# Sums of weights and low parts of activations made by accumulating DMAs, in a transformer block that multiplies in three passes

## The chip, the cores and the metric

The kernel runs on one core of one Trainium2 chip. The metric is the device time of one execution in microseconds; the time before is the median of three runs. The core has TensorE (PE, with its weight loads PEld), VectorE (DVE), ScalarE (ACT), GpSimd (POOL) and SyncE (SP), and 16 DMA engines that carry out the transfers which SP, ACT and POOL issue.

## What is computed

One encoder block on 256 tokens of width 2048, all in float32 (cut to what matters here):

```python
proj = x @ w_in                       # retention q, k, v, gate; latent q, kv, rope key
mix  = concat(retention(proj), latent_attention(proj)) @ w_out
x1   = layer_norm(ALPHA * x + mix, ln1_g, ln1_b)
h    = square(relu(x1 @ w_up)) @ w_down        # w_up 2048 x 8192, w_down 8192 x 2048
out  = layer_norm(ALPHA * x1 + h, ln2_g, ln2_b)
```

The up product (`w_up`) and the down product (`w_down`) are where the change works. The third place with seven-product pairs, the retention projection, keeps its own way of building sums, apart from one sign.

## The kernel before

**Three products for one.** TensorE multiplies in a reduced-precision float32 format, `F32R`. Each operand is split into a high part (rounded to that format by ScalarE, line 389) and a low part, the rest (a subtraction on VectorE, line 390). A product is then high x high + high x low + low x high: three matmuls of 128 x 512, one after the other into the same accumulator. Weights arrive from DRAM 1 MB at a time in one of three `raw` buffers (loads issued by SP), and their high and low parts stand in five slots of 128 x 1024 (`hi`, `lo`). A raw buffer is loaded again when the weights three jobs back have been read; a slot is filled again when TensorE is done with it.

**Pairs.** A job is two 128-deep slices of a weight matrix, 1024 columns wide, against 256 tokens: a 2 x 2 block product (two slices, two halves of 512 columns, two halves of 128 tokens). Done plainly (`pair_products`, line 353) it takes eight products, 24 matmuls. Some jobs use Winograd's form of Strassen's scheme (`seven_products`, line 441): seven products, 21 matmuls, bought with sums of weights (`first`, `second`, `third` in `weights_pair`, lines 398, 404, 408, all VectorE) and sums of tokens (`token_sums`, lines 364 to 369). `SEVEN` lists which jobs of the two down passes are sevens, `UP_SEVEN` those of the up blocks: 2 in block 1 and 4 in each of blocks 2 to 7. Products that several outputs share gather in four more accumulators (`mb`), which `up_gather` and `add_sums` combine afterwards.

**Down passes.** The down product runs twice over all 32 pairs, once for each half of the output columns: pass 0, then pass 1 in another order of blocks. Two pairs use one block of 512 activations. `r_split` makes a block's high part `rhl[:, 0]` on ScalarE (line 1233) and its low part `rhl[:, 1]` on VectorE (line 1237); two such tiles take turns. Pass 0 writes the low part of blocks 0 to 13 to DRAM (`r_keep`, line 1243, a DMA on GpSimd's queue), and pass 1 reads it back (line 1235). Token sums of six pairs (`STORED`) made in pass 0 are kept for pass 1.

**Order.** The program is scheduled by hand: each engine executes in the order in which the code issues. While TensorE's work for a job is being written, `unit()` issues the next pieces of jobs to come (`next_piece`), as far as slots allow, in the order of `SEVEN_PARTS`: s0 token sums, s1 to s3 weight sums, w0 to w3 the splits. `load_ahead` issues the raw loads. So an instruction that waits on VectorE holds all later pieces on VectorE.

Of the kernel before, what the change touches and what calls it, by code (L numbers as in the profile page):

```python
# [14 lines left out]
P = 128  # L15
# [27 lines left out]

SEVEN_PARTS = ('s0', 's1', 'w0', 's2', 'w2', 's3', 'w1', 'w3')
X1_AT = ((1, 2), 1)
UP_STEP = 1
# [18 lines left out]
NSLOT = 5  # L65
LO_KEPT = range(14)
X_AFTER = {0: (1, 1), 1: (2, 2), 3: (4, 4), 6: (8, 4), 10: (12, 4)}

# [24 lines left out]
class Job:  # L93


    def __init__(self, load, pieces, slotted):
        self.load = load
        self.pieces = pieces
        self.slotted = slotted
        self.slots = None  # L100
        self.left = None
        self.seven = False
        self.held = False
# [8 lines left out]
def kernel(  # L112
# [44 lines left out]
    holders = []  # L157
    state = {"dma": 0, "job": 0, "unit": 0, "pause": 0, "heads": 0}
# [18 lines left out]
    def next_piece(force):  # L177
        while state["job"] < len(jobs) and not left(jobs[state["job"]]):
            state["job"] += 1
        if state["job"] == len(jobs):  # L180
            return False
        job = jobs[state["job"]]
        if job.held:
            return False
        load_ahead(state["job"])
        i = job.left[0]
# [174 lines left out]
    def token_sums(r0, r1, st, v):  # L361


        nc.vector.tensor_add(st[:, 0], r0[:, P:], r1[:, P:])
        nc.vector.tensor_sub(st[:, 1], st[:, 0], r0[:, 0:P])
        nc.vector.tensor_sub(st[:, 2], r0[:, 0:P], r0[:, P:])
        nc.vector.tensor_sub(st[:, 3], r1[:, 0:P], st[:, 1])
        nc.scalar.copy(v[:, :, 0], st)
        return lambda: nc.vector.tensor_sub(v[:, :, 1], st, v[:, :, 0].bitcast(F32))

    def weights_pair(name, load, half, columns, sums=None, seven=False, into=None):

# [23 lines left out]
        def first():  # L396
            a, b, t13 = columns(job, extra["t13"])
            nc.vector.tensor_sub(t13, a, b)
            if sums:
                job.rest()  # L400

# [4 lines left out]
        def third():  # L406
            b21 = half(job, 1, 0, 4)
            nc.vector.tensor_sub(shaped(extra["t4"], b21), b21, half(job, 0, 4, 8))

        job.load = lambda: load(job)  # L410
        job.seven = seven
        if not seven:
            job.pieces = [lambda e=e: split(e, half(job, e, 0, 8)) for e in range(2)]
            job.slots = [e if into is None or into[e] is None else None for e in range(2)]
        else:
            parts = {"s0": token_part, "s1": first, "s2": second, "s3": third,
                     "w0": lambda: split(0, half(job, 1, 0, 8)), "w1": lambda: split(1, half(job, 0, 0, 8)),
                     "w2": lambda: split(2, extra["t13"]), "w3": lambda: split(3, extra["t4"], 512)}
            job.pieces = [parts[p] for p in SEVEN_PARTS]
            job.slots = [int(p[1]) if p[0] == "w" else None for p in SEVEN_PARTS]  # L420
        job.hi, job.lo = [None] * 4, [None] * 4
# [7 lines left out]
    def seven_products(job, x, k, sums, cb, mb, first, last, done=None):  # L429
        for a, w, o, pb, alone in ((("x", 1, 0), 0, 0, cb[0][0], False), (("s", 3), 0, 512, cb[0][1], False),  # L430
                                   (("s", 0), 2, 0, mb[2], True), (("s", 2), 2, 512, mb[3], True),
                                   (("x", 0, 0), 1, 0, mb[0], True), (("s", 1), 1, 512, mb[1], True),
                                   (("x", 1, 1), 3, 0, cb[1][0], False)):
            use_slot(job, w)
# [7 lines left out]
            if o or w == 3:  # L442
                free(job, (w,))
                if done and w == 1:
                    side.append(done)
# [98 lines left out]
    def up_pair(b, kp):  # L544
        def load(job):
            raw = raw_tile(job, f"raw_wu{b}_{kp}")
            nc.sync.dma_start(raw.rearrange("p (f c) -> p f c", f=8),
                              w_up[8 * b:8 * b + 8, :, kp * 256:(kp + 1) * 256].rearrange("f p c -> p f c"))
# [4 lines left out]
        def columns(job, t):  # L553
            v = job.raw.rearrange("p (f e c) -> p f e c", f=8, e=2)
            return (v[:, 4:8].rearrange("p f e c -> p e f c"), v[:, :, 0].rearrange("p (j f) c -> p j f c", j=2),
                    t.rearrange("p (j f c) -> p j f c", j=2, c=P))

        return weights_pair(f"wu{b}_{kp}", load, half, columns, None, kp in UP_SEVEN[b])

    def down_pair(p, pair, into=None, seven=None):  # L560
        def load(job):
            raw = raw_tile(job, f"raw_wd{p}_{pair}")
            nc.sync.dma_start(raw.rearrange("p (e c) -> p e c", e=2),
                              w_down[2 * pair:2 * pair + 2, :, p * 1024:(p + 1) * 1024].rearrange("e p c -> p e c"))

        def half(job, e, i, j):
# [7 lines left out]

        def columns(job, t):
            return (job.raw.rearrange("p (e j c) -> p e j c", e=2, j=2)[:, :, 1],
                    job.raw[:, 0:1024].rearrange("p (j c) -> p j c", j=2), t.rearrange("p (j c) -> p j c", j=2))

        return weights_pair(f"wd{p}_{pair}", load, half, columns, None if seven is None or p == 1 and pair in STORED else sums, seven is not None, into)

# [645 lines left out]
    def r_split(b, keep=None):  # L1226
# [7 lines left out]
        if b in lo_kept:  # L1234
            nc.gpsimd.dma_start(t[:, 1].rearrange("p k t -> p (k t)"), lo_kept[b])
        else:
            nc.vector.tensor_sub(t[:, 1], r, t[:, 0].bitcast(F32))
# [71 lines left out]
    def up_gather(mb):  # L1309
# [9 lines left out]
        nc.vector.tensor_add(g[2], g[2], g[1])  # L1319
        nc.vector.tensor_add(g[1], g[1], g[3])  # L1320
        yield
        nc.vector.tensor_add(g[3], g[3], g[2])

# [72 lines left out]
    def add_sums(p, mb):  # L1396
# [13 lines left out]
        plus(0, 1, v)  # L1410
        nc.vector.tensor_add(v, v, p5)
        yield
        plus(1, 1, v)
        nc.vector.tensor_add(u, u, p5)
        yield
# [194 lines left out]
```

## Time and profile before

| what | value |
|---|---|
| median of 3 runs | 1100.75 us (1100.7 to 1100.85) |
| the profiled execution's own time | 1100.88 us |
| its span in the trace | 1099.1 us |
| granted TensorE clock | 0.999 |
| busy: PE, PEld | 1091.1 us (99%), 912.1 us (83%) |
| busy: DVE, ACT, POOL | 955.4 us (87%), 656.7 us (60%), 24.7 us (2%) |
| DMA moved | 231.78 MB, mean 211 GB/s |

The span is the time from the first to the last instruction of the program in the trace. In a timeline row the first number is the start in us from the span's beginning, the second how long the instruction (or the merged row) took; matmuls overlap in the pipeline, so what one costs is the distance from start to start. `u`, `v` and `d`, `s` are accumulators of up and down products, plain and shared; `t` and `ut` hold weight sums, `sx` token sums, `xm` the sums ahead of their split, `rr` the activations.

### The profile page before, as it was taken

The numbers are of one execution on the slowest core, as the hardware profiler recorded it, in microseconds if no ns is written. First come the engines' busy times: TensorE is split into PE (matmuls) and PEld (weight loads), VectorE is DVE, ScalarE is ACT, GpSimd is POOL, SyncE is SP. The second block draws the span as 40 slices with busy tenths as digits, with TensorE's granted clock in tenths as the row PEclk, the third lists the DMA queues.
The fourth block names the chain that finished last, engine by engine and source line by source line (L and its number), as shares of the span: only waits on it lengthen the run. The fifth ranks groups of instructions, "written<-read, shape, count | busy, mean of one in ns | idle before, by whom it ended". The sixth has DMA issues, their size and how long they took to land.

```text
span 1099.1 us, 13768 instructions
## 1 busy us (share of the span) xinstructions
PE 1091.1 (99%) x5145; PEld 912.1 (83%) x5145; DVE 955.4 (87%) x1304; ACT 656.7 (60%) x847; POOL 24.7 (2%) x46
## 2 busy tenths in 40 slices
PE   9999999999999999999999999999999999999997
PEld 8888888888888889888888888888888888888885
DVE  7878779889785777889999999999899999999985
ACT  4545556546463455467777677776666663666660
POOL 0000000000000000000000000000000000000000
PEclk9999999999999999999999999999999999999999
DMA  8655364535266544666656756757677876777792
GB/s 286 243 201 188 138 225 171 222 115 208 109 230 230 216 176 154 194 200 197 213 171 196 234 165 192 230 181 271 205 249 253 260 239 220 264 238 263 255 336 97
DMA packets 97026, 231.78 MB, mean 211 GB/s; under 512 B 4672, under 2 KB 63040, under 8 KB 89152
## 3 DMA queue, kind: packets, MB, share of 16 engines
q1 hardware_dynamic: 92496, 215.64, 57.6%
q0 software_dynamic: 4032, 14.68, 3.9%
q8 instruction: 40, 0.66, 0.2%
q10 hardware_dynamic: 432, 0.59, 0.2%
q14 instruction: 26, 0.21, 0.1%
HBM read 221.46 MB, written 9.44 MB: 210 GB/s over the span
## 4 chain that ended last, share of the span: by engine, by line
PE 97%; DVE 1%; DMA 1%; issue 0%; ACT 0%; POOL 0%; SPq 0%; DVEq 0%
PE d L353 21%; PE u L353 15%; PE r L353 12%; PE o L353 8%; PE v L441 6%; PE s L441 5%; PE u L441 5%; PE m L353 5%; PE d L441 4%; PE rs L441 2%; PE up L924 2%; PE pu L924 2%; PE r L441 1%; PE ut L1353 1%; PE pv L353 1%; PE up L930 1%
## 5 line engine op out<-in xcount | busy, mean ns | idle before, releaser
L353 PE MATMUL d<-hi_wd,rhl 128*128 128x512 f32 x632 | 174.7, 390 | 0.0
L390 DVE TENSOR_TENSOR lo_wd<-raw_wd,hi_wd 128x1024 fp32r<-128x1024 f32 x125 | 150.4, 1220 | 19.9 <-ACT hi_wd L389 19.5
L389 ACT CAST hi_wd<-raw_wd 128x1024 fp32r<-128x1024 f32 x125 | 129.3, 1051 | 56.1 <-DVE raw_wd L404 17.8
L390 DVE TENSOR_TENSOR lo_wu<-raw_wu,hi_wu 128x1024 fp32r<-128x1024 f32 x112 | 135.5, 1220 | 12.0 <-ACT hi_wu L389 10.9
L353 PEld LDWEIGHTS d<-hi_wd,rhl 128*128 128x128 f32 x632 | 118.4, 188 | 24.3
L389 ACT CAST hi_wu<-raw_wu 128x1024 fp32r<-128x1024 f32 x112 | 117.7, 1055 | 34.5 <-PE u L353 10.6
L353 PE MATMUL u<-hi_wu,x1hl 128*128 128x512 f32 x480 | 137.0, 394 | 0.0
L353 PE MATMUL r<-hi_ret,xhl 128*128 128x512 f32 x384 | 110.2, 397 | 0.0
L353 PEld LDWEIGHTS u<-hi_wu,x1hl 128*128 128x128 f32 x480 | 88.3, 188 | 17.2
L353 PE MATMUL d<-lo_wd,rhl 128*128 128x512 f32 x316 | 97.7, 389 | 0.0
L353 PEld LDWEIGHTS r<-hi_ret,xhl 128*128 128x128 f32 x384 | 71.0, 188 | 14.1
L390 DVE TENSOR_TENSOR lo_ret<-raw_ret,hi_ret 128x1024 fp32r<-128x1024 f32 x64 | 76.1, 1218 | 6.9 <-ACT hi_ret L389 6.7
L389 ACT CAST hi_ret<-raw_ret 128x1024 fp32r<-128x1024 f32 x64 | 65.9, 1052 | 25.6 <-PE r L353 14.7
L353 PE MATMUL u<-lo_wu,x1hl 128*128 128x512 f32 x240 | 74.2, 390 | 0.0
L353 PEld LDWEIGHTS d<-lo_wd,rhl 128*128 128x128 f32 x316 | 59.3, 188 | 12.4
L353 PE MATMUL r<-lo_ret,xhl 128*128 128x512 f32 x192 | 59.5, 391 | 0.0
L353 PE MATMUL o<-hi_wo,mix 128*128 128x512 f32 x208 | 57.5, 393 | 0.0
L441 PE MATMUL v<-hi_wu,us 128*128 128x512 f32 x156 | 56.5, 389 | 0.0
L353 PEld LDWEIGHTS u<-lo_wu,x1hl 128*128 128x128 f32 x240 | 45.0, 188 | 9.6
L441 PE MATMUL s<-hi_wd,sx 128*128 128x512 f32 x126 | 45.6, 389 | 0.0
L353 PEld LDWEIGHTS o<-hi_wo,mix 128*128 128x128 f32 x208 | 38.7, 188 | 7.8
L240 ACT CAST hi_wo<-raw_wo 128x1024 fp32r<-128x1024 f32 x26 | 27.0, 1054 | 27.4 <-PE o L353 19.1
(341 smaller groups left out, 2210.6 us busy)
## 6 DMA issues: line engine op xcount, KB each, us to landing
raw_wu<-in_w_up SPq DMA_DIRECT2D x64, 1024.0 KB, 5.4
raw_wd<-in_w_down SPq DMA_DIRECT2D x64, 1024.0 KB, 5.9
raw_ret<-in_w_ret SPq DMA_DIRECT2D x32, 1024.0 KB, 4.8
raw_wo<-in_w_out SPq DMA_DIRECT2D x16, 1024.0 KB, 4.8
raw_mla<-in_w_mla SPq DMA_DIRECT2D x14, 672.0 KB, 5.1
lo_kept<-rhl POOLq DMA_DIRECT2D x14, 512.0 KB, 4.1
rhl<-lo_kept POOLq DMA_DIRECT2D x13, 512.0 KB, 3.6
raw_qk<-in_w_qk SPq DMA_DIRECT2D x8, 640.0 KB, 3.9
```

Of the source, the lines that this page charges most:

```text
L240: nc.scalar.copy(hi[:, o:e], r)
L353: nc.tensor.matmul(accs[j][:, :w], x_part, w_part[:, a:a + w], start=first and fst and i == 0, stop=last and lst and i == len(steps) - 1)
L389: nc.scalar.copy(h, src)
L390: nc.vector.tensor_sub(l, src, h.bitcast(F32))
L441: nc.tensor.matmul(pb, x_part, w_part, start=alone and first and fst, stop=alone and last and lst)
L924: nc.tensor.matmul(pb, hi[:, a:a + P], hl[:, k0 + i], start=first and i == ks[0], stop=last and i == ks[-1])
L930: nc.tensor.matmul(pb[:, 0:S], lo[:, a:a + P], hl[:, k0 + i, 0:S], start=False, stop=last and i == ks[-1])
L1353: nc.tensor.transpose(pts[i][:, f * P:(f + 1) * P], gathered[i][:, f * P:(f + 1) * P], ident)
```

## The change

In the up blocks and both down passes a seven's first weight sum (the second half of the columns plus the first half, of the first slice) is now made by a DMA that GpSimd issues: it reads the first half again from DRAM and adds it to the second half where that lies in the raw buffer, once the load has landed. The sums are rearranged so that two VectorE subtractions follow from it instead of three, and the products inside a seven stand in another order. In pass 0 the low part of blocks 1 to 15 is made by ScalarE writing minus the high part and a GpSimd DMA adding the activations to it. Pass 0 has eleven sevens instead of ten, and both lists of positions are new; `STORED` is not changed.

```diff
-SEVEN = ((4, 7, 9, 12, 14, 17, 19, 22, 25, 27), (2, 4, 6, 8, 10, 12, 14, 16, 18, 20, 22))
+SEVEN = ((4, 6, 8, 11, 13, 16, 18, 21, 23, 25, 27), (3, 5, 7, 9, 11, 13, 15, 17, 19, 21, 23))
 SEVEN_PARTS = ('s0', 's1', 'w0', 's2', 'w2', 's3', 'w1', 'w3')
+ADDED_PARTS = ('s0', 's2', 's3', 'w0', 'w1', 'w2', 'w3')
+LO_ADDED = range(1, 16)
...
+    def add_ahead():
+        while state["added"] and jobs.index(state["added"][0][0]) <= state["job"] + 1:
+            _, dst, src = state["added"].pop(0)
+            nc.gpsimd.dma_start(dst, src, accum_op=ALU.add)
...
+        def added_second():
+            b22 = half(job, 1, 4, 8)
+            nc.vector.tensor_sub(shaped(extra["t4"], b22), half(job, 0, 4, 8), b22)
+            if sums:
+                job.rest()
+
+        def added_third():
+            low = columns(job)
+            t4, t13 = extra["t4"], extra["t13"].rearrange("p (e c) -> p e c", e=2)
...
+            nc.vector.tensor_sub(t13, low, t4.unsqueeze(1).to_broadcast(low.shape))
...
+            steps = ((("x", 1, 0), 0, 0, cb[0][0], False), (("s", 3), 0, 512, cb[0][1], False),
+                     (("x", 0, 0), 1, 0, mb[0], True), (("s", 0), 1, 512, mb[2], True),
+                     (("s", 2), 2, 0, mb[3], True), (("x", 1, 1), 2, 512, cb[1][0], False),
+                     (("s", 1), 3, 0, mb[1], True))
...
     def up_pair(b, kp):
...
+            if job.seven:
+                state["added"].append((job, half(job, 0, 4, 8),
+                                       w_up[8 * b:8 * b + 4, :, kp * 256:kp * 256 + P].rearrange("f p c -> p f c")))
...
     def down_pair(p, pair, into=None, seven=None):
...
+            if job.seven:
+                state["added"].append((job, raw[:, 512:1024], w_down[2 * pair, :, p * 1024:p * 1024 + 512]))
...
     def r_split(b, keep=None):
...
+        elif b in LO_ADDED:
+            nc.scalar.activation(t[:, 1], t[:, 0].bitcast(F32), AF.Copy, scale=-1.0)
+            nc.gpsimd.dma_start(t[:, 1].rearrange("p k t -> p (k t)"), r.rearrange("p k t -> p (k t)"), accum_op=ALU.add)
```

The rest of the diff turns signs around: `up_gather` and `add_sums` subtract where they added, and `token_sums` has its third sum negated.

GpSimd's queue at the start of the first down pass. Before, it holds only the stores of low parts (`lo_kept`, with `rhl` the activations of a block):

```order
L1243 DMA lo_kept0_6550<-rhl_6501 128x1024
L1243 DMA lo_kept1_6658<-rhl_6552 128x1024
L1243 DMA lo_kept2_6733<-rhl_6660 128x1024
L1243 DMA lo_kept3_6824<-rhl_6735 128x1024
L1243 DMA lo_kept4_6911<-rhl_6826 128x1024
```

And now (`raw_wd0_4` is the raw buffer of pair 4 of pass 0):

```order
L1279 DMA lo_kept0_6550<-rhl_6498 128x1024
L1271 DMA rhl_6552<-rr0_3778 128x1024
L176 DMA raw_wd0_4_6522<-in_w_down 128x512
L1279 DMA lo_kept1_6659<-rhl_6552 128x1024
L1271 DMA rhl_6661<-rr0_3778 128x1024
L176 DMA raw_wd0_6_6624<-in_w_down 128x512
L1279 DMA lo_kept2_6736<-rhl_6661 128x1024
L1271 DMA rhl_6738<-rr0_3778 128x1024
L176 DMA raw_wd0_8_6756<-in_w_down 128x512
```

Between two stores stand the add of the next block's low part and, for most blocks, the add of one weight half.

VectorE in the second down pass, around one seven whose token sums are not stored and the pair behind it. Before (`xm` the token sums, `t13` and `ut` the weight sums):

```order
L367 TENSOR_TENSOR xm_1590<-rr0_3778,xm_1590 128x128
L398 TENSOR_TENSOR t13_3805<-raw_wd1_0_8163 128x1024
L369 TENSOR_TENSOR sx_6543<-xm_1590,sx_6543 128x4x128
L390 TENSOR_TENSOR lo_wd1_0_0_8258<-raw_wd1_0_8163,hi_wd1_0_0_8257 128x1024
L404 TENSOR_TENSOR raw_wd1_0_8163<-raw_wd1_0_8163,t13_3805 128x512
L390 TENSOR_TENSOR lo_wd1_0_2_8269<-t13_3805,hi_wd1_0_2_8268 128x1024
L408 TENSOR_TENSOR ut_3780<-raw_wd1_0_8163 128x512
L390 TENSOR_TENSOR lo_wd1_0_1_8277<-raw_wd1_0_8163,hi_wd1_0_1_8276 128x1024
L390 TENSOR_TENSOR lo_wd1_0_3_8293<-ut_3780,hi_wd1_0_3_8292 128x512
L390 TENSOR_TENSOR lo_wd1_1_0_8311<-raw_wd1_1_8211,hi_wd1_1_0_8310 128x1024
```

And now, at the seven that has taken its place (pair 1 instead of pair 0):

```order
L376 TENSOR_TENSOR xm_1590<-rr0_3778,xm_1590 128x128
L419 TENSOR_TENSOR ut_3780<-raw_wd1_1_8239 128x512
L378 TENSOR_TENSOR sx_6543<-xm_1590,sx_6543 128x4x128
L429 TENSOR_TENSOR t13_3805<-raw_wd1_1_8239,ut_3780 128x1024
L399 TENSOR_TENSOR lo_wd1_1_0_8347<-raw_wd1_1_8239,hi_wd1_1_0_8346 128x1024
L399 TENSOR_TENSOR lo_wd1_1_1_8351<-raw_wd1_1_8239,hi_wd1_1_1_8350 128x1024
L399 TENSOR_TENSOR lo_wd1_1_2_8358<-t13_3805,hi_wd1_1_2_8357 128x1024
L399 TENSOR_TENSOR lo_wd1_1_3_8377<-ut_3780,hi_wd1_1_3_8376 128x512
L399 TENSOR_TENSOR lo_wd1_2_0_8396<-raw_wd1_2_8295,hi_wd1_2_0_8395 128x1024
```

Both weight sums now stand ahead of all four low parts, and the first of them (line 419) reads what the DMA has added.

ScalarE in the first down pass, around a block's activations: before, one cast (line 1233) between the casts of weights,

```order
L389 CAST hi_wd0_15_0_7154<-raw_wd0_15_7053 128x1024
L1233 CAST rhl_7160<-rr1_3779 128x1024
L389 CAST hi_wd0_15_1_7169<-raw_wd0_15_7053 128x1024
L389 CAST hi_wd0_16_0_7181<-raw_wd0_16_7086 128x1024
L389 CAST hi_wd0_16_1_7191<-raw_wd0_16_7086 128x1024
```

and now a second pass over the same tile behind it (line 1270), ahead of the add:

```order
L398 CAST hi_wd0_15_1_7160<-raw_wd0_15_7054 128x1024
L377 CAST sx_6543<-xm_1590 128x4x128
L1266 CAST rhl_7179<-rr1_3779 128x1024
L1270 ACTIVATE rhl_7179<-rhl_7179 128x1024
L398 CAST hi_wd0_16_0_7189<-raw_wd0_16_7113 128x1024
```

The weight casts that followed the activations at once now follow one operation later.

More of the change, by code (lines that the diff above doesn't have):

```diff
@@ L102, in __init__ @@
         self.seven = False
+        self.plus = False
         self.held = False
@@ L157 @@
     holders = []
-    state = {"dma": 0, "job": 0, "unit": 0, "pause": 0, "heads": 0}
+    state = {"dma": 0, "job": 0, "unit": 0, "pause": 0, "heads": 0, "added": []}
     def load_ahead(upto):
@@ L185, in next_piece @@
         load_ahead(state["job"])
+        add_ahead()
         i = job.left[0]
@@ L369, in token_sums, with weights_pair @@
         return lambda: nc.vector.tensor_sub(v[:, :, 1], st, v[:, :, 0].bitcast(F32))
-    def weights_pair(name, load, half, columns, sums=None, seven=False, into=None):
+    def weights_pair(name, load, half, columns, sums=None, seven=False, into=None, plus=False):
         job = Job(None, [], into is None or None in into)
@@ L398, in first @@
             nc.vector.tensor_sub(t13, a, b)
-            if sums:
-                job.rest()
         def second():
@@ L415, in weights_pair @@
         else:
-            parts = {"s0": token_part, "s1": first, "s2": second, "s3": third,
+            parts = {"s0": token_part, "s1": first, "s2": added_second if plus else second,
+                     "s3": added_third if plus else third,
                      "w0": lambda: split(0, half(job, 1, 0, 8)), "w1": lambda: split(1, half(job, 0, 0, 8)),
                      "w2": lambda: split(2, extra["t13"]), "w3": lambda: split(3, extra["t4"], 512)}
-            job.pieces = [parts[p] for p in SEVEN_PARTS]
-            job.slots = [int(p[1]) if p[0] == "w" else None for p in SEVEN_PARTS]
+            names = ADDED_PARTS if plus else SEVEN_PARTS
+            job.pieces = [parts[p] for p in names]
+            job.slots = [int(p[1]) if p[0] == "w" else None for p in names]
         job.hi, job.lo = [None] * 4, [None] * 4
@@ L429, in seven_products @@
     def seven_products(job, x, k, sums, cb, mb, first, last, done=None):
[L430 to L433, printed above, removed]
+        if job.plus:
+            steps = ((("x", 1, 0), 0, 0, cb[0][0], False), (("s", 3), 0, 512, cb[0][1], False),
+                     (("x", 0, 0), 1, 0, mb[0], True), (("s", 0), 1, 512, mb[2], True),
+                     (("s", 2), 2, 0, mb[3], True), (("x", 1, 1), 2, 512, cb[1][0], False),
+                     (("s", 1), 3, 0, mb[1], True))
+        else:
+            steps = ((("x", 1, 0), 0, 0, cb[0][0], False), (("s", 3), 0, 512, cb[0][1], False),
+                     (("s", 0), 2, 0, mb[2], True), (("s", 2), 2, 512, mb[3], True),
+                     (("x", 0, 0), 1, 0, mb[0], True), (("s", 1), 1, 512, mb[1], True),
+                     (("x", 1, 1), 3, 0, cb[1][0], False))
+        for a, w, o, pb, alone in steps:
             use_slot(job, w)
@@ L443, in seven_products @@
                 free(job, (w,))
-                if done and w == 1:
+                if done and w == (3 if job.plus else 1):
                     side.append(done)
@@ L548, in load, with columns @@
                               w_up[8 * b:8 * b + 8, :, kp * 256:(kp + 1) * 256].rearrange("f p c -> p f c"))
+            if job.seven:
+                state["added"].append((job, half(job, 0, 4, 8),
+                                       w_up[8 * b:8 * b + 4, :, kp * 256:kp * 256 + P].rearrange("f p c -> p f c")))
         def half(job, e, i, j):
             return job.raw.rearrange("p (f e c) -> p f e c", f=8, e=2)[:, i:j, e]
[L553 to L558, printed above, removed]
+        def columns(job):
+            return job.raw.rearrange("p (f e c) -> p f e c", f=8, e=2)[:, 0:4].rearrange("p f e c -> p e f c")
+        return weights_pair(f"wu{b}_{kp}", load, half, columns, None, kp in UP_SEVEN[b], plus=True)
     def down_pair(p, pair, into=None, seven=None):
@@ L573, in sums, with columns @@
             return token_sums(r0, r1, st, sums_of(seven, pair))
[L575 to L579, printed above, removed]
+        def columns(job):
+            return job.raw.rearrange("p (e j c) -> p e j c", e=2, j=2)[:, :, 0]
+        return weights_pair(f"wd{p}_{pair}", load, half, columns, None if seven is None or p == 1 and pair in STORED else sums, seven is not None, into, True)
     def sums_of(q, pair):
```

14 lines of the change are left out of this document (9 added, 5 removed).

## The prediction

> **What bounds the kernel now.** I read the page first, then who waits on TensorE, then TensorE's own rows, and last the engines behind it, stage by stage.
>
> The page says that TensorE works nearly the whole span and that 97% of the chain that ended last is TensorE; VectorE is the next fullest engine.
>
> ```profile
> span 1099.1 us, 13768 instructions
> ...
> PE 1091.1 (99%) x5145; PEld 912.1 (83%) x5145; DVE 955.4 (87%) x1304; ACT 656.7 (60%) x847; POOL 24.7 (2%) x46
> ...
> PE 97%; DVE 1%; DMA 1%; issue 0%; ACT 0%; POOL 0%; SPq 0%; DVEq 0%
> ```
>
> A busy share can hide short stops, so the waits of TensorE are the second view. All that it waited for is this (engine, line, releaser, total us, times, longest):
>
> ```profile
> PE last L1513 <- ACT xm L1511: 1.5, 1, 1.5
> PE m L616 <- POOL warm L613: 1.0, 1, 1.0
> PE m L353 <- DVE lo_mla L241: 0.5, 1, 0.5
> PE x1t L1084 <- DVE xm L1078: 0.2, 1, 0.2
> PE up L1114 <- DVE x1hl L1099: 0.2, 1, 0.2
> ```
>
> None lies in the up or down passes, which the change touches. So VectorE's 87% costs nothing today: work taken off it buys time only through the matmuls that the new seven saves. What a seven is worth stands in TensorE's rows around one seven of the first down pass (line 441) and the two ordinary pairs after it (line 353; start us, us, ...):
>
> ```profile
> 854.95 0.39 PE L441 MATMUL d<-hi_wd,rhl 128*128 128x512 f32 x1
> ...
> 859.71 0.62 PE L353 MATMUL d<-hi_wd,rhl 128*128 128x512 f32 x2
> ...
> 870.59 0.39 PE L441 MATMUL d<-hi_wd,rhl 128*128 128x512 f32 x1
> ```
>
> The seven's 21 matmuls take 859.71 - 854.95 = 4.76 us; two pairs of 24 take 10.88 us, 5.44 each. Both are 0.227 us a matmul, start to start. By stage: first down pass, second down pass, and the up blocks with what stands just ahead of them (us, then PE, PEld, DVE, ACT, POOL busy with counts, clock, DMA share, GB/s):
>
> ```profile
> 744.00:918.00 174.00, 174.00 (x777) 144.10 (x776) 164.96 (x203) 111.46 (x127) 7.66 (x14) 1.00 0.74 245
> 918.00:1060.00 142.00, 142.00 (x628) 117.48 (x627) 132.44 (x158) 90.39 (x100) 7.41 (x14) 1.00 0.75 261
> 440.00:744.00 304.00, 304.00 (x1411) 252.70 (x1410) 281.88 (x321) 212.54 (x267) 0.00 (x0) 1.00 0.63 197
> ```
>
> VectorE is at 95%, 93% and 93% there, the DMA engines at 74%, 75% and 63%: nothing stops TensorE, but two resources are close.
>
> **The sum on TensorE.** The first down pass gets 11 sevens for 10: 24 - 21 = 3 matmuls fewer, 3 x 0.227 = 0.68 us. The second keeps eleven, the up blocks their 26. The other order of products inside a seven has the same 21 matmuls. So TensorE alone gives 1100.88 - 0.68 = 1100.2 in the profiled execution's own time, which stands 0.13 above the median of the runs, 1100.75; on the median 1100.07. All else adds, if anything.
>
> **VectorE's work.** Its rows in the second down pass, from the sums of one seven that is not stored to those of the next (the first four operations build the token sums, L398 and L404, L408 the weight sums):
>
> ```profile
> 968.88 0.28 DVE L364 TENSOR_TENSOR xm<-rr 128x128 f32<-128x128 f32 x1
> ...
> 969.81 1.22 DVE L398 TENSOR_TENSOR t<-raw_wd 128x1024 f32<-128x1024 f32 x1
> 970.95 0.68 DVE L369 TENSOR_TENSOR sx<-xm,sx 128x512 fp32r<-128x512 f32 x1
> 971.55 1.22 DVE L390 TENSOR_TENSOR lo_wd<-raw_wd,hi_wd 128x1024 fp32r<-128x1024 f32 x1
> 972.68 0.69 DVE L404 TENSOR_TENSOR raw_wd<-raw_wd,t 128x512 f32<-128x512 f32 x1
> 973.29 1.22 DVE L390 TENSOR_TENSOR lo_wd<-t,hi_wd 128x1024 fp32r<-128x1024 f32 x1
> ...
> 978.73 1.23 DVE L390 TENSOR_TENSOR lo_wd<-raw_wd,hi_wd 128x1024 fp32r<-128x1024 f32 x1 [0.67 <-ACT hi_wd L389]
> 979.87 0.28 DVE L364 TENSOR_TENSOR xm<-rr 128x128 f32<-128x128 f32 x1
> ```
>
> Start to start, 1024 wide costs 1.14 us, 512 wide 0.61, the token sums 0.93 and their low part 0.60. A changed seven has one 512-wide and one 1024-wide subtraction (half of it a repeated operand, taken at the same price) where there were one 1024-wide and two 512-wide: 0.61 less, 26 times in the up blocks. In the first down pass the fifteen low parts go too, 15 x 1.14 = 17 us less. The second pass is the other way: six of its sevens used sums stored in the first pass, but the new positions share none with the list of stored pairs, so eleven token sums are built, not five, as this group counts them:
>
> ```profile
> L369 DVE TENSOR_TENSOR sx<-xm,sx 128x512 fp32r<-128x512 f32 x5 | 3.4, 684 | 0.0
> ```
>
> That is 6 x (0.93 + 0.60) = 9.2 more against 11 x 0.61 = 6.7 less: 132.4 + 2.5 = 134.9 of 142 us, 95%. It fits. By the cycle above, 979.87 - 968.88 = 10.99 for a seven and a pair, of which 0.67 is a wait: 9.7 to 10.4 after the change, against 4.76 + 5.44 = 10.20 on TensorE. The upper end would lag 0.2 us eleven times, 2 us, and VectorE's lead is about that: the low part begun at 971.55 is done at 972.7, and TensorE starts this seven at 974.71:
>
> ```profile
> 974.71 0.39 PE L441 MATMUL d<-hi_wd,rhl 128*128 128x512 f32 x1
> ```
>
> Between those ends I take no stop: the 0.67 of waiting is not work.
>
> **The new DMAs.** No accumulating DMA is in the trace. The nearest rows are GpSimd's 512 KB copies between on-chip and DRAM memory; an added weight half has 256 KB. Here are the stores, then one copy back, issued at 955.0, 0.3 us after a weight load, and that load itself; and the load of the seven of the VectorE rows above:
>
> ```profile
> L1243 POOL DMA_DIRECT2D lo_kept<-rhl x14: 531/531/744, 754.5 to 886.5; - x14
> ...
> DMA to landing us min/median/max: 2.9/4.1/5.9
> ...
> L1235 POOL DMA_DIRECT2D rhl<-lo_kept x1: 528/528/528, 955.0 to 955.0; - x1
> ...
> DMA to landing us min/median/max: 6.8/6.8/6.8
> ...
> L563 SPq DMA_DIRECT2D raw_wd<-in_w_down x1: 368/368/368, 954.7 to 954.7; - x1
> ...
> DMA to landing us min/median/max: 6.1/6.1/6.1
> ...
> L563 SPq DMA_DIRECT2D raw_wd<-in_w_down x1: 368/368/368, 958.8 to 958.8; - x1
> ...
> DMA to landing us min/median/max: 5.5/5.5/5.5
> ```
>
> So an add may take from below 2.9 us (about 2.1, with half the bytes) to 6.8, where a load shares the engines and the copy lands 1 us behind it. The wait it puts in stands at VectorE's first weight subtraction: these weights landed at 964.3 and were first read at 969.81, 5.5 us later. Behind that instruction queue VectorE's other low parts, and TensorE waits for those. An add of the median copy's 4.1 us is hidden; one of 6.8 is 1.3 us late. I take 4 to 5, nearest the median row, since only some adds meet a fresh load, so no wait.
>
> On sharing, that row shows a copy issued just behind a load landing last. [...] The measurement decides the range.
>
> In the up blocks an add moves 512 pieces of 512 bytes, not 128 rows. In block 5 the load of the last seven is issued at 643.8 and lands 5.4 us later, at 649.2; its first product is the second matmul of the row below, at about 658.2.
>
> ```profile
> L547 SPq DMA_DIRECT2D raw_wu<-in_w_up x1: 368/368/368, 643.8 to 643.8; - x1
> ...
> DMA to landing us min/median/max: 5.4/5.4/5.4
> ...
> 657.95 0.61 PE L441 MATMUL u<-hi_wu,x1hl 128*128 128x512 f32 x2
> ```
>
> Behind the add stand 0.61 + 1.14 + 1.14 = 2.9 us of VectorE before the first low part, so about 6.0 us remain for it. If writing the pieces out costs four times the 0.53 us of a 128-row issue, the range shifts by 1.6 to 3.7-8.4; I take 5, hidden, as GpSimd has nothing else there.
>
> For the low parts of the activations the cover is the time until TensorE opens the block. Before, in the tenth block:
>
> ```profile
> 854.25 1.05 ACT L1233 CAST rhl<-rr 128x1024 fp32r<-128x1024 f32 x1
> 855.98 1.22 DVE L1237 TENSOR_TENSOR rhl<-rr,rhl 128x1024 fp32r<-128x1024 f32 x1
> ```
>
> TensorE starts that block at 859.71 and reads the low part 0.9 later, at 860.6. After: two ScalarE passes (2.1), then a 512 KB add of 2.9 to 6.8: 859.3 to 863.2, if ScalarE comes no sooner. It can: the buffer is free when TensorE ends the block before last, at 849.5, and ScalarE was late because VectorE was. Freed of 17 us, I expect it 2 us or more sooner, and no stop. ScalarE's own added 15 x 1.05 = 16 us fit in its 174 - 111.
>
> **Rivals.**
> A, forecast: every add lands under cover; 1100.1.
> B, late adds in the second down pass (the other sign). VectorE stops at its first weight subtraction whenever an add takes over 5.5 us; past the 2 us of lead that goes to TensorE, eleven times. At 6.8 plus 0.2 of wake-up: 11 x 1.5 - 2 = 14 us, 1114; with half of them late, 1106. For it speaks the 6.8 row, against it the median.
> C, the DMA engines fill in the first down pass:
>
> ```profile
> q1 hardware_dynamic: 9130, 35.17, 61.4%
> q0 software_dynamic: 2016, 7.34, 12.2%
> ```
>
> Fourteen stores took 12.2% of 174 us, 1.52 each. Fifteen low parts add 15 x 1.52 = 23 us and eleven halves 11 x 0.76 = 8 (0.74 x 174 = 129 us of work becomes 160 in 173); if reading the target doubles the price, 191 of 173, an end of 18 us more: 1118. It decides from about 1.4 times a copy's price.
> D, late 512-byte adds in six up blocks: at 8.4 us, 6 x 2.4 = 14 us, 1114.
> E, faster by more than 2.2 us: ten matmuls' worth would have to go, and TensorE has no wait to lose. GpSimd's adds being all hidden, or not helping at all, both end in A.
>
> On issue, the rows show GpSimd's DMA instructions at 531 ns median and 744 at most with VectorE at 95%. [...]
>
> **How the numbers follow.** A 0.60, B 0.16, C 0.13, D 0.08, E 0.03. The predicted time is A's, 1100.1. The low end is A less a little, 1099.8. The high end is 1112, which leaves out the upper third of B, C and D (0.12) and E. Faster by over 0.2% (2.2 us, about what a measurement of this kernel can tell from no change) is E, 0.03; within it A, 0.60; slower B, C, D, 0.37. A alone: 1099.8 to 1102.9.
>
> **What would show it.** Right: 3 matmuls fewer in the first down pass, no new waits on TensorE in the up and down passes, VectorE near 85% in the first (165 - 17 - 6 + 5 for the added seven, of 173) and 95% in the second pass, adds landing in 4 to 5 us. Wrong: TensorE waiting for VectorE's low weights, with VectorE waiting for an accumulating DMA at the first weight subtraction (B, D); a DMA share over 0.95 in the first pass, or TensorE waiting for a block's low part (C).

## The result: 6.6% slower

| what | before | after |
|---|---|---|
| median of the runs | 1100.72 us (4 runs) | 1171.94 us (4 runs, 1171.24 to 1177.47) |
| ratio | 1 | 1.0658 (95% interval 1.0625 to 1.0691) |
| profiled execution, its span | 1100.88, 1099.1 us | 1171.33, 1169.6 us |
| up blocks | 345.8 us | 356.1 us |
| first down pass | 169.2 us | 216.0 us |
| second down pass | 150.8 us | 164.8 us |

The stages run from the start of TensorE's first matmul on the second 1 MB of up weights (408.0 us before, so the first 47 us are still block 0, which has no sevens), on down pair 0, on the second pass's first pair, and (the end) on pair 20 in the second pass; the same marks serve for all kernels below. The profiled executions differ by 70.5 us: 10.3, 46.8 and 13.9 more in these stages, 0.6 less ahead of them, and the same behind.

The page of after: span, busy times, the chain's shares, the granted clock in 40 slices, the two large DMA queues.

```profile
span 1169.6 us, 13948 instructions
...
PE 1116.7 (95%) x5142; PEld 922.3 (79%) x5142; DVE 926.9 (79%) x1281; ACT 671.7 (57%) x871; POOL 90.5 (8%) x109
...
PEclk9999999999999999999999999999889889999999
...
q1 hardware_dynamic: 92496, 215.64, 54.2%
q0 software_dynamic: 23088, 35.13, 14.7%
...
PE 51%; DMA 21%; DVE 15%; issue 9%; ACT 3%; POOL 0%; POOLq 0%; DVEq 0%; ACTq 0%
```

The chain was 97% TensorE; now DMA and VectorE hold 36% of it. VectorE has 28.5 us less to do, and no slice of the clock was below 9 before. TensorE's waits in after (total us, times, longest) name the places:

```profile
PE d L362 <- DMA rhl<-rr: 19.9, 7, 5.3
PE d L472 <- DVE lo_wd L399: 14.6, 10, 3.1
PE u L472 <- DVE lo_wu L399: 7.2, 8, 1.5
PE d L472 <- DMA rhl<-rr: 3.7, 2, 2.7
```

Two kinds: a block's low part that the adding DMA has not finished (23.6 us, first pass only), and a seven's first low weights (21.8 us). Who holds VectorE there is in the list of all waits:

```profile
DVE ut L419 <- DMA raw_wd<-in_w_down: 65.4, 19, 8.4
```

So VectorE stands at its first weight subtraction, as rivals B and D have it. The DMA issues (KB each, median us from issue to landing) and the issue of an up add (busy us, mean ns):

```profile
raw_wd<-in_w_down SPq DMA_DIRECT2D x64, 1024.0 KB, 6.9
rhl<-rr POOLq DMA_DIRECT2D x15, 512.0 KB, 8.2
lo_kept<-rhl POOLq DMA_DIRECT2D x14, 512.0 KB, 5.9
raw_wu<-in_w_up POOLq DMA_DIRECT2D x26, 256.0 KB, 5.9
raw_wd<-in_w_down POOLq DMA_DIRECT2D x22, 256.0 KB, 7.4
...
L176 POOL DMA_DIRECT2D raw_wu<-in_w_up x26 | 33.6, 1291 | 303.1 <-DVE lo_wu L399 102.3
```

In the median an added weight half takes 7.4 us in the down passes and a low part 8.2, both above the 6.8 us that the prediction had as the upper end. One late block shows how both kinds hang together (rows of DVE, ACT, POOL and PE in the first pass; start us, us, in brackets the idle time before):

```profile
895.90 0.69 DVE L419 TENSOR_TENSOR ut<-raw_wd 128x512 f32<-128x512 f32 x1 [7.94 <-DMA raw_wd<-in_w_down]
...
895.96 1.05 ACT L398 CAST hi_wd<-raw_wd 128x1024 fp32r<-128x1024 f32 x1 [6.39 <-DMA raw_wd<-in_w_down]
...
899.39 1.04 ACT L1266 CAST rhl<-rr 128x1024 fp32r<-128x1024 f32 x1
...
901.83 0.85 POOL L1271 DMA_DIRECT2D rhl<-rr  x1 [8.12 <-ACT rhl L1270]
902.45 1.11 POOL L176 DMA_DIRECT2D raw_wd<-in_w_down  x1
...
904.64 0.61 PE L362 MATMUL d<-lo_wd,rhl 128*128 128x512 f32 x2
910.54 2.07 PE L362 MATMUL d<-hi_wd,rhl 128*128 128x512 f32 x4 [5.28 <-DMA rhl<-rr]
```

ScalarE's queue holds the cast of the added weight half, and behind it the block's activations. The weight add lands at 895.9, so the activations come at 899.4, the add of their low part at 901.8, and TensorE, there at 904.9, gets it at 910.5. GpSimd's queue closes the ring: the next weight add stands there behind the low part's add and leaves at 902.45, 3.8 us after its load landed (898.7). Four of the eleven weight adds of the first pass left so, 2.6 to 5.8 us after their load; the others 0.6 to 0.7. What such a stop does to the clock stands in these windows (us; PE, PEld, DVE, ACT, POOL busy, clock, DMA share, GB/s): the stop, what follows, and then the pace as before:

```profile
904.90:909.80 4.90, 0.36 (x2) 0.00 (x0) 1.38 (x5) 1.56 (x2) 0.00 (x0) 1.00 1.07 250
909.80:916.70 6.90, 6.16 (x15) 4.82 (x16) 3.34 (x4) 1.85 (x2) 0.57 (x1) 0.51 0.47 179
916.70:923.00 6.30, 6.30 (x29) 5.20 (x28) 5.70 (x7) 4.67 (x6) 1.73 (x2) 1.00 0.62 179
```

For 6.9 us after the stop the clock is at half and a matmul costs 0.43 us, not 0.227. In the first pass 37.5 us ran so: stops of 30.1 us, and some 16 us more in the slow matmuls behind them, are nearly all of the 46.8.

### The profile page after: what moved, and what is told of

It is laid out like the page before. It is cut to its first block, busy times and chain, and to the rows that moved or that the text cites. A ratio compares the mean times of both kernels' runs of the same rounds, so it can differ in the third digit from the quotient of the medians.

```text
span 1169.6 us, 13948 instructions
## 1 busy us (share of the span) xinstructions
PE 1116.7 (95%) x5142; PEld 922.3 (79%) x5142; DVE 926.9 (79%) x1281; ACT 671.7 (57%) x871; POOL 90.5 (8%) x109
## 4 chain that ended last, share of the span: by engine, by line
PE 51%; DMA 21%; DVE 15%; issue 9%; ACT 3%; POOL 0%; POOLq 0%; DVEq 0%; ACTq 0%
PE d L362 12%; DMA raw_wu<-in_w_up 12%; PE r L362 11%; PE o L362 7%; DMA raw_wd<-in_w_down 7%; DVE lo_wu L399 6%; PE m L362 4%; DMA rhl<-rr 3%; DVE lo_wd L399 2%; DVE t L429 2%; PE rs L472 2%; DVE ut L419 2%; PE pu L957 2%; PE r L472 1%; PE s L472 1%
## 5 line engine op out<-in xcount | busy, mean ns | idle before, releaser
L362 PE MATMUL d<-hi_wd,rhl 128*128 128x512 f32 x616 | 180.6, 408 | 19.9 <-DMA rhl<-rr 19.9
L362 PEld LDWEIGHTS d<-hi_wd,rhl 128*128 128x128 f32 x616 | 120.9, 198 | 48.6 <-DMA rhl<-rr 22.9
L399 DVE TENSOR_TENSOR lo_wu<-raw_wu,hi_wu 128x1024 fp32r<-128x1024 f32 x112 | 132.5, 1218 | 6.8 <-ACT hi_wu L398 6.8
L419 DVE TENSOR_TENSOR ut<-raw_wd 128x512 f32<-128x512 f32 x22 | 15.2, 692 | 65.4 <-DMA raw_wd<-in_w_down 65.4
L176 POOL DMA_DIRECT2D raw_wu<-in_w_up x26 | 33.6, 1291 | 303.1 <-DVE lo_wu L399 102.3
L472 PE MATMUL s<-hi_wd,sx 128*128 128x512 f32 x132 | 48.6, 396 | 0.0
```

The source lines that it names most:

```text
L176: nc.gpsimd.dma_start(dst, src, accum_op=ALU.add)
L362: nc.tensor.matmul(accs[j][:, :w], x_part, w_part[:, a:a + w], start=first and fst and i == 0, stop=last and lst and i == len(steps) - 1)
L399: nc.vector.tensor_sub(l, src, h.bitcast(F32))
L419: nc.vector.tensor_sub(shaped(extra["t4"], b22), half(job, 0, 4, 8), b22)
L472: nc.tensor.matmul(pb, x_part, w_part, start=alone and first and fst, stop=alone and last and lst)
```

## The experiments

### One part at a time: x1, x2, x3, x4

The theory at first (L): the low parts' adds cost most. The rival (W): the weight adds do. x1 takes the low parts back to VectorE, x4 also the up blocks; x2 and x3 are the kernel before with one part of the change, x3 with its eleventh seven at position 29, which is not one of the change's positions.

```diff
 x1 (after):   -LO_ADDED = range(1, 16)          +LO_ADDED = ()
 x4 (x1):      the up blocks' sums by VectorE, as before
 x2 (before):  +    elif b in LO_ADDED: (ScalarE's pass and the adding DMA, blocks 1 to 15)
 x3 (before):  -SEVEN = ((..., 25, 27), ...      +SEVEN = ((..., 25, 27, 29), ...
```

> The changed kernel with the low parts of the first down pass made by VectorE again; the weight sums by adding DMAs, the eleven sevens and the positions stay. Theory L (the low-part adds are the main cause: they take 8.2 us at the median, TensorE waits for them at the start of blocks, and its clock halves after such stops): the first down pass falls from 216 us to about 175 to 180, the clock stays at 1.0 there, the total is about 1130 to 1137. Rival W (the weight adds are the root: ScalarE's casts of the added half wait for them, in order, and the block's activations come late behind those): the first down pass stays above 200 us, the total above 1155.

> The kernel before with one thing added: low parts of blocks 1 to 15 by ScalarE and an adding DMA in the first down pass. No weight adds, ten sevens, the old positions. Theory L: the first down pass takes 195 us or more instead of 169, the total 1125 or more, with half-clock stretches of 3.4 us after the stops. Rival W: without weight adds ScalarE reaches the activations in time and the low parts land under cover: 1100 to 1104.

> The kernel before with one more seven in the first down pass, at its 30th job, and no DMA added. Three matmuls fewer at 0.227 us: if VectorE, at 95% of that pass, still has room for 5 us more, 1100.0 to 1100.2. If VectorE is already full there, TensorE waits and it is 1102 or more.

> As x1_weights_only, and the up blocks as before, so weight adds in the two down passes alone. If the 9.6 us that the up blocks lost come from their own 512-byte adds, this is 9 to 10 us under x1_weights_only, under theory L at 1121 to 1128; if they come from something that the down passes share, no difference.

| kernel | median us | ratio (95% interval) | up blocks | first pass | second pass |
|---|---|---|---|---|---|
| x1 weights only | 1151.07 | 1.0442 (1.0413 to 1.0471) | 357.2 | 190.5 | 167.9 |
| x2 low parts only | 1127.68 | 1.0229 (1.0202 to 1.0256) | 345.8 | 197.0 | 150.8 |
| x3 eleven only | 1106.68 | 1.0051 (1.0036 to 1.0066) | 345.8 | 168.5 | 156.8 |
| x4 down weights only | 1139.76 | 1.0347 (1.0332 to 1.0363) | 345.8 | 190.4 | 169.4 |

TensorE's waits, first of x1, then of x2:

```profile
PE d L472 <- DVE lo_wd L399: 25.7, 17, 3.1
PE u L472 <- DVE lo_wu L399: 8.3, 9, 1.5
```

```profile
PE d L354 <- DMA rhl<-rr: 19.5, 5, 7.3
```

Each kind costs by itself, the weight adds (with the new positions) 50 us and the low parts 26.5. So L was right on x2, and on x1 both missed: 1151 us and 190.5 lie between L's range and W's. The up adds alone are 11.3 us (x1 against x4). x3 shows the gain that was promised, 168.5 for 169.2 us in the first pass, and where it goes: 5.1 us of stops at the start of the second pass, where VectorE is busy for 25.8 of 26.0 us.

```profile
921.00:947.00 26.00, 21.24 (x90) 16.38 (x89) 25.83 (x33) 10.55 (x12) 0.55 (x1) 1.00 0.60 193
```

### The price of adding: x5, x7, x11

The same DMAs without the addition: the same bytes are copied over the target. The sums are left out of these kernels.

```diff
-            nc.gpsimd.dma_start(dst, src, accum_op=ALU.add)
+            nc.gpsimd.dma_start(dst, src)
```

x5 is x4 with this, x11 is x1, and x7 is x2 with the low part's DMA changed in the same way.

> The weight adds of the two down passes alone (x4), but the DMA copies the first half over the second instead of adding it: same bytes, same queue, same waits, and the sum itself is left out. In x4 a 2 KB packet of an add took 178 ns and the adds landed about 7.1 us after their issue, of which some 3.6 us passed before the first packet, behind a raw load issued just ahead. Theory R (raw-buffer loop): the time is set by load 8.4 + add 7.1 + VectorE 8.6 us = 24.1 us from the load of one seven to the load of the seven after the next, for two cycles of which TensorE needs 20.4. A copy saves only the packets' part, about 0.7 us in the add and as much in the load beside it: 22.7, 1.15 us lost a cycle, second down pass about 162 us, time 1122 to 1130. Rival P (the price of accumulation): without it the copy lands in about 4.1 us like the stores before, and the stalls go: second pass 151 to 153, time 1101 to 1108.

> The low parts of the activations alone (x2), but the DMA writes the activations over the tile instead of adding them: same bytes, queue and waits, the subtraction is left out. In x2 a 4 KB packet of an add took 328 ns against 174 of a copy, the median add 8.6 us. Rival P (price): the copy lands in about 4 to 6 us, the cover of 5.3 us from issue to first use holds nearly always, and the first down pass goes back to 169 to 174 us, time 1100.5 to 1106. Theory Q (queueing behind loads and ScalarE's order): the DMA's packets save some 1.2 us of 8.6, the long ones that meet two loads stay late; first pass 183 to 192, time 1113 to 1123.

> All weight adds (x1) as plain copies over the second half, the addition left out, to price accumulation in the up blocks, where an add has 512 pieces of 512 bytes: issue 1.29 us, landing 5.9 us in the median, up blocks 357.2 us with and 345.8 without adds. If the price of accumulating is the cause there (packets of some 65 ns, and the longer issue), the up blocks go back to 346 to 348 us. If the number of pieces is the cause, whatever is done to them, they stay at 354 to 357. The down passes should repeat x5: 183 and 157. Time 1122 to 1136.

Measured: x5 1122.99 us (1.0199, 1.0185 to 1.0213), 183.2 and 157.2 us in the two passes; x7 1117.63 (1.0156, 1.0140 to 1.0171), 185.1 in the first; x11 1124.65 (1.0216, 1.0199 to 1.0233), 347.0 in the up blocks. x7 is where theory Q had it, x11 where price had it; x5 has R's time, but its second pass lies between R's 162 and P's 151 to 153. The low part's DMA in x2 and x7, and the down adds in x4 and x5 (median us to landing last):

```profile
rhl<-rr POOLq DMA_DIRECT2D x15, 512.0 KB, 8.6
```

```profile
rhl<-rr POOLq DMA_DIRECT2D x15, 512.0 KB, 5.4
```

```profile
raw_wd<-in_w_down POOLq DMA_DIRECT2D x22, 256.0 KB, 7.3
```

```profile
raw_wd<-in_w_down POOLq DMA_DIRECT2D x22, 256.0 KB, 5.5
```

Without the addition a low part lands 3.2 us sooner (of 8.6) and a weight half 1.8 (of 7.3). On the path that is 10.1 us from x2 to x7, two fifths of the low parts' loss, and 26.4 from x1 to x11, about half of the weights'. In x2 and x7 the packets of that queue are the same (6192), so that difference is the addition's. In x1 and x11 they are not; the queue of GpSimd's DMAs there (packets, MB, share of 16 engines):

```profile
q0 software_dynamic: 20928, 27.27, 11.4%
```

```profile
q0 software_dynamic: 7872, 27.27, 7.4%
```

The plain copies went out in packets of 4 KB, the adds in pieces of 2 KB (down) and 512 bytes (up). So x11 takes away the addition and the small pieces together, and does not tell which of the two its expectation asked about is the cause; nor does x5. The packets' own times allow an estimate: per KB an adding packet takes 82 ns at 4 KB (328), 89 at 2 KB (178) and 130 at 512 bytes (65), a copying one 44 at 4 KB (174). By that the addition is most of it for the down halves, and the pieces are about half of it for the up halves. Together they are nearly all of what the up blocks lost (357.2 to 347.0), and there the issue on GpSimd is part of it, x1 ahead of x11 (ns min/median/max):

```profile
L176 POOL DMA_DIRECT2D raw_wu<-in_w_up x26: 1282/1283/1478, 464.4 to 746.9; - x26
```

```profile
L176 POOL DMA_DIRECT2D raw_wu<-in_w_up x26: 747/747/942, 464.7 to 735.9; - x26
```

What stays with plain copies is in part the waiting in line. In x2 a low part's add was issued at 806.1, 0.6 us behind a raw load. The shares of the DMA queues in the 4 us after, and in the next 4 (packets, MB, share of 16 engines):

```profile
q1 hardware_dynamic: 199, 0.81, 82.1%
q0 software_dynamic: 10, 0.03, 2.2%
```

```profile
q0 software_dynamic: 137, 0.50, 63.1%
q1 hardware_dynamic: 151, 0.55, 37.4%
```

The load (q1) goes first, the add (q0) mostly after it, and this one landed after 11.0 us.

### Why a seven is late: x6, x9, x13, x15

Two theories here. R: load, add and VectorE's work form a loop through the three raw buffers, longer than TensorE's work. C (H in x6, where VectorE's order was the whole cost): the add lands too long after the load, however far apart the sevens stand.

```diff
 x6 (x4):  -ADDED_PARTS = ('s0', 's2', 's3', 'w0', 'w1', 'w2', 'w3')
           +ADDED_PARTS = ('s0', 'w0', 's2', 's3', 'w1', 'w2', 'w3')
 x9 (x4):  +SEVEN = ((4, 8, 12, 16, 20, 24, 27), (3, 7, 11, 15, 19, 23))
 x13 (x9), x15 (x4):
           -            nc.gpsimd.dma_start(t[:, 1]..., lo_kept[b])
           +            nc.scalar.dma_start(t[:, 1]..., lo_kept[b])
```

> x4 with the split of the slice that no add touches (w0) written ahead of the two weight subtractions, so its low part no longer queues on VectorE behind the instruction that waits for the add. Rival H (VectorE's order is the whole cost): TensorE stalled in x4 at this low part only, so the stalls go, second down pass about 152 us, first about 170, time 1101 to 1106. Theory R (the raw buffers' loop): one 1.13 us low part leaves the part behind the add, 23.0 us for two cycles against 20.4; 1.3 us a seven stay, now at another low part: second pass about 163 us, time 1120 to 1130.

> The weight adds of the down passes alone (x4), but with sevens further apart: 7 in the first pass, 6 in the second, at every fourth pair. Fewer sevens cost TensorE 3 matmuls each: the passes are then 171.3 and 154.2 us without a stall. In x4 the second pass ran at 12.0 us for a seven and a pair where TensorE needs 10.2. Theory R (a loop through the three raw buffers: load, add, VectorE's work, next load, 24.1 us for 2 x 10.2): with three plain pairs between two sevens only one add falls into a turn, the loop has slack and the stalls of the sevens go; second pass 154 to 156, first 171 to 176, time 1106 to 1114. Rival C (cover: an add lands 7 us after its load and the weights are wanted 5.5 us after it, however far the sevens stand apart): 6 x 1.6 = 10 us stay in the second pass, 164, and as much in the first, 182; time 1125 or more.

> x9 (a seven at every fourth pair) with one DMA on another queue: the second pass reads a block's low part back by a DMA that ScalarE issues, not GpSimd. In x9 TensorE waited 12.0 us in five stops for that copy, which stood on GpSimd's queue right behind the add of a seven, and not once in that pass for a seven's own weights. If the order on GpSimd's queue was the cause, these stops go: second pass 154 to 158 against 172.0, time 1126 to 1133, and theory R holds for the weights (sevens far apart are not late). Rival: the copy is late because the DMA engines serve it behind the load and the add, whoever issues it: second pass 168 to 172, time 1140 or more.

> The same move of the read-back to ScalarE's queue in x4, where every second pair of the second pass is a seven and TensorE waited for the sevens' low weights, not for the copy. Theory R: the loop load, add, VectorE, load stays as long, second pass 166 to 170 (169.4 in x4), time 1136 to 1141. Rival: the adds are late because they queue on GpSimd behind the copies: second pass 152 to 158, time 1122 to 1130.

| kernel | median us | ratio (95% interval) | first pass | second pass |
|---|---|---|---|---|
| x6 untouched slice first | 1141.45 | 1.0372 (1.0358 to 1.0386) | 191.1 | 171.5 |
| x9 every fourth | 1145.99 | 1.0408 (1.0392 to 1.0424) | 193.0 | 172.0 |
| x13 every fourth, read-back on ScalarE | 1140.99 | 1.0363 (1.0349 to 1.0377) | 193.4 | 165.2 |
| x15 x4, read-back on ScalarE | 1134.27 | 1.0307 (1.0290 to 1.0324) | 189.6 | 161.7 |

x6 missed both. At all sevens of the second pass but the first two the stop moved to the next low part, 1.64 to 1.71 us long each time, whatever the add did (VectorE waited for adds only 0.8 us in that pass). ScalarE's and VectorE's rows at one of them:

```profile
1063.53 0.62 ACT L377 CAST sx<-xm 128x512 fp32r<-128x512 f32 x1 [2.41 <-DVE xm L376]
1064.05 2.15 ACT L398 CAST hi_wd<-raw_wd 128x1024 fp32r<-128x1024 f32 x2
...
1065.13 1.23 DVE L399 TENSOR_TENSOR lo_wd<-raw_wd,hi_wd 128x1024 fp32r<-128x1024 f32 x1 [1.64 <-ACT hi_wd L398]
1066.27 0.68 DVE L419 TENSOR_TENSOR ut<-raw_wd 128x512 f32<-128x512 f32 x1
```

The slice that needs no add needs ScalarE's cast, and that stands behind the cast of the token sums, which VectorE has just finished. So now VectorE waits 1.64 us for ScalarE, every time, with the weight subtractions behind. The turned order put one wait in the place of another.

x9 gave C's time for another reason. No seven of its second pass was late; five blocks were, by their low parts read back from DRAM:

```profile
PE d L362 <- DMA rhl<-lo_kept: 12.0, 5, 3.6
```

GpSimd's rows show why: the copy stands in order behind the add, and the add waits for its load. (14.54 us idle ahead of it; the bracket names VectorE, but the load landed at 972.6, and the add left 0.7 us later.)

```profile
973.35 0.85 POOL L176 DMA_DIRECT2D raw_wd<-in_w_down  x1 [14.54 <-DVE lo_wd L399]
973.91 0.85 POOL L1267 DMA_DIRECT2D rhl<-lo_kept  x1
```

With the copy on ScalarE's queue (x13) these stops go but for one, and four of six sevens are late instead by 1.2 to 2.2 us: 165.2 us, near C's 164. That misses both of x13's own ranges, R's 154 to 158 and the rival's 168 to 172, and part of it is half clock (3.4 us) and the one late copy. At one of the late sevens (GpSimd, VectorE, TensorE):

```profile
998.15 0.85 POOL L176 DMA_DIRECT2D raw_wd<-in_w_down  x1 [21.52 <-DVE xm L374]
...
1005.25 0.69 DVE L419 TENSOR_TENSOR ut<-raw_wd 128x512 f32<-128x512 f32 x1 [6.76 <-DMA raw_wd<-in_w_down]
...
1008.87 0.50 PE L472 MATMUL d<-lo_wd,rhl 128*128 128x512 f32 x1 [1.00 <-DVE lo_wd L399]
```

Its load was issued at 991.6, when a buffer came free. From there: 5.9 us to land (997.5), 0.7 to issue the add, 7.1 for it, 3.4 of VectorE to the end of the first low part, at 1008.7; TensorE wanted it at 1007.7, 16.1 us after the buffer came free. So R, as a loop that distance between sevens would open, fell. At this seven the buffers gave the load a lead of some 16 us, and the add made the way 17. x15 is between its two theories: the read-back's place on GpSimd's queue is 7.7 us of x4's 18.6 in the second pass, the rest stays.

### Is there a version that wins? x8, x10, x12, x14

The kernel before with the eleventh seven of the first pass elsewhere, and low parts by DMA only where the trace of before has cover and no fresh load.

```diff
 x8:  +SEVEN = ((3, 4, 7, ..., 25, 27), ...
 x10: +SEVEN = ((4, 7, ..., 27, 29), ...        +LO_ADDED = (3, 7, 8, 12)
 x12: +SEVEN = ((2, 4, 7, ..., 25, 27), ...
 x14: +SEVEN = ((3, 4, 7, ..., 25, 27), ...     +LO_ADDED = (1,)
```

> The kernel before with the eleventh seven of the first down pass at position 3 instead of 29 (nothing by DMA). At 29 it put 5.6 us of VectorE work in front of the pass change, and TensorE stopped there for 5.1 us (x3). VectorE idles about 5 us between 760 and 800 us, because slots are full, and only 0.1 to 0.4 of each 10 us later. If that room takes the seven: 3 matmuls x 0.227 = 0.68 us less, 1100.5. If the lateness is carried to the pass change or TensorE waits for the seven at position 4: 1101 to 1106.

> The kernel before with the eleventh seven at position 29 (x3) and the low parts of four blocks by the adding DMA: 3, 7, 8 and 12, which in the trace of before have 6.3 to 7.5 us between the moment of the add and TensorE's first use, and no raw load issued in the 2 us ahead of that moment. In x2, where all fifteen were added, the adds that met a load issued 0.5 us ahead landed after 10 to 11 us, the undisturbed ones after 4 to 5. Theory Q (an add is late where it queues behind a load): the four are hidden, VectorE has 4 x 1.14 = 4.6 us less to do before the pass change, and most of x3's 5.1 us stop there goes; 1100.2 to 1102.5. Rival: every add disturbs the raw loads, or the freed time ends as idle time before the pass change: 1105 or more.

> The kernel before with the eleventh seven of the first down pass at position 2. At 29 it stopped TensorE for 5.1 us at the pass change (x3), at 3 for 1.5 us at the seven of position 4 (x8). At 2 there are two plain pairs... one plain pair between it and the next seven, so the stop should go: first pass 168.5, time 1100.5. If instead TensorE waits for this seven's own weights, whose work can only begin when the up blocks are done: 1 to 4 us of stop, 1101 to 1104.

> The kernel before with the eleventh seven of the first pass at position 3 (x8) and the low part of block 1 alone by the adding DMA. In x8 TensorE stopped 1.5 us at the seven of position 4, while VectorE was full from 752 to 771 us, block 1's low part (1.14 us) in it, and ScalarE idle 6 us just ahead. That add has 10 us of cover in the trace of before. If it is hidden, the stop shrinks to about 0.4 us and the saving of 0.68 us shows: 1100.3 to 1101.2. If ScalarE's added pass, or the order of its casts, holds the seven: 1101.5 to 1103.

| kernel | median us | ratio (95% interval) | first pass | second pass |
|---|---|---|---|---|
| x8 at 3 | 1102.56 | 1.0014 (1.0005 to 1.0022) | 170.5 | 150.9 |
| x10 at 29, four adds | 1108.32 | 1.0063 (1.0050 to 1.0075) | 168.9 | 158.8 |
| x12 at 2 | 1105.69 | 1.0041 (1.0029 to 1.0054) | 172.3 | 151.3 |
| x14 at 3, one add | 1101.12 | 1.0003 (0.9994 to 1.0012) | 169.3 | 150.8 |

In x10 the four chosen adds landed in 4.9 us in the median and none was late: away from loads they are hidden. But the stop at the pass change stayed whole, because the freed time came too early: VectorE idled from 815 to 845 us (25.8 us of work in 30.0, 29.3 in x3) and was as full as in x3 from 900 on (21.9 of 22.0 in both). x10's second pass is 2.0 us longer than x3's: a half-clock window of 3.4 us followed its second stop, and none followed x3's.

```profile
PE s L442 <- DVE lo_wd L391: 4.7, 2, 2.6
```

x12 stopped 2.2 us at the seven itself, and came out above both of its ranges. The wait was not for the seven's weights but for ScalarE (line 1347), which was still emptying the accumulators of the last up block:

```profile
PE s L441 <- ACT rr L1347: 2.5, 3, 2.1
```

x14 freed VectorE just where x8 was late (1.5 us), and that stop is gone; but 0.6 us of shorter gaps in the same pass eat the three matmuls. It ties with the kernel before. None of these kernels beats it.

## Why the prediction was wrong

**The matmuls: right.** Three fewer were 0.7 us in x3's first pass, and TensorE's count fell from 5145 to 5142. **VectorE's work: right as a sum, useless as a saving.** 28.5 us less (some 31 by the prediction's terms) were bought on an engine that held nobody up, and paid for on the path.

**The step that failed: the add's latency, "I take 4 to 5, nearest the median row, since only some adds meet a fresh load".** Measured medians are 7.4, 5.9 and 8.2 us for down weights, up weights and low parts. So the "no wait" that followed from it fell too. The choice between the ends was wrong: the row that an add resembles was the copy issued just behind a load (6.8), not the median (4.1); even the plain copies of x5 took 5.5. An add becomes possible when a load lands, and other loads are in the air or leave at that time; in x4's second pass nine of eleven adds saw their first packet only 3.3 to 4.6 us after their issue began. The row's 6.8 was no upper end either, as the next term shows.

**The doubled price** ("if reading the target doubles the price") was put into rival C as a condition, and is nearly so: 328 ns for a 4 KB packet that adds against 174 for one that copies (178 for 2 KB that add). One of C's signs came, TensorE waiting for a block's low part; its cause did not: over the first pass the DMA engines were not full (share 0.83, beside the 0.91 clock in the row below). They were full for short stretches, such as the stop above (1.07), when a load and adds were in flight together. So the price lengthened single waits, not the pass as a whole.

```profile
766.00:981.00 215.00, 186.70 (x748) 149.41 (x747) 144.16 (x182) 121.36 (x136) 29.63 (x39) 0.91 0.83 242
```

**Rival B** had the place, the sign and the price: 14 us forecast (14.5 by its own terms), 13.9 found in the second pass, although 7.7 of x4's loss there hung on GpSimd's queue, which B did not have; that the two numbers are so close is in part luck. B's 0.2 us of wake-up stands in no row: VectorE started 0.02 us after an add had landed, and what B left out is the 0.5 to 0.8 us from a load's landing to the add's issue. **Rival D** too: up to 14 forecast, 10.3 found. With a room of 6.0 us and a 5.9 us median add, 8 of 26 sevens stopped TensorE. Both had chances of 0.16 and 0.08, and were priced as alternatives; in fact B, D and late low parts came together.

**The low parts:** "ScalarE 2 us sooner" fell. In x2, with no weight add in the way, ScalarE still began a block 4.7 us after its buffer was free (850.4), as before (849.5 to 854.25), since its casts wait for VectorE's sums (2.59 and 1.03 us of idle time in the 4 us ahead). In the rows of after above it came later still, behind the added weights. These adds were estimated at 859.3 to 863.2 against a need at 860.6, and the early end was chosen.

**What no rival had: the clock.** Over all traces of this case, in the up blocks and down passes, 75 stops of TensorE of 1.0 to 1.9 us brought no slow clock; of 51 longer ones 36 were followed, at the latest 1.5 us after their end, by one to three windows of 3.4 us at half clock. In the first pass of after that is some 16 us: eight stops, five of them with one window behind them and three with two. The shortest stop that sufficed was 2.0 us (in after 2.05, the distance between two matmuls' starts less 0.227; the longest there without a slow clock was 1.71).

**Sharing of the DMA engines:** the copy issued 0.3 us behind a load landed 1 us after it (6.8 us). In x2 the add issued 0.6 us behind a load fared worse: its queue took 2.2% of the engines in the first 4 us and the load's 82.1%, then 63.1% and 37.4%, and the add landed after 11.0 us. No run here shows how an engine chooses between the two queues.

**GpSimd's issue:** 0.86 us for a 128-row add and 1.28 for 512 pieces, 0.54 and 0.75 without the addition, and in x4 nearly the same each time while VectorE worked (0.855 to 0.887 over 22 adds). The rise comes from the addition and the pieces.

Left open: what the new positions and the six more token sums of the second pass cost by themselves, since no run has them with VectorE's own weight sums (with plain copies, x5, the second pass is still 6.4 us longer than before); how the price of the weight adds divides between the addition and the small pieces; why the losses of x1 and x2 add up to a little more than after's (76 for 71 us); and how much of x4's first pass (190.4 us) is GpSimd's queue, which also carries the stores there.

## What to carry to other kernels

A DMA that adds is priced at twice a copy's bytes (328 ns for 4 KB here, against 174) and put behind whatever load is in flight (2.2% of the engines for 4 us, against 82.1%), so its latency is taken from the worst row of a copy issued beside a load, and is compared with the lead that the buffers give from the moment a buffer is freed. Work taken off an engine that nobody waits for buys nothing (28.5 us of VectorE's here), while an instruction that waits for a DMA at the head of an in-order queue (VectorE's sums, ScalarE's casts, GpSimd's own DMAs) holds all that stands behind it (VectorE stood 65.4 us at its first weight subtraction in after). A stop of TensorE of 2 us or more should be counted at up to 3 us extra, for the half clock that may follow it (36 of 51 here; 15 matmuls at 0.43 us behind the stop shown above).

## What was not expected of the hardware

- An accumulating packet of 4 KB took 328 ns against 174 for a copy; the issue on GpSimd took 0.86 us against 0.54. Without the addition the same 27.27 MB went out in 7872 packets, not 20928.
- A DMA issued 0.6 us behind a 1 MB load got 2.2% of the engines for 4 us, and the load 82.1%.
- Stops of TensorE between 1.9 and 3 us were enough for 3.4 us at half clock in 19 of 33 cases, and none of 75 shorter ones, of 1.0 to 1.9 us, was.
